# A hybrid decoder step on one core: decay banks written by kind, the last head's old states read in the gate stage, states in head order, stored SiLUs one at a time

## The chip, the core and the metric

The kernel is one program on one core of a Trainium2 chip. The metric is the device time of one execution in microseconds (us), as the median of the runs. The engines are named as in the profile: PE is TensorE with its matmuls (PEld its weight loads), DVE is VectorE, ACT is ScalarE, POOL is GpSimd, and SP is the engine whose instruction queue issues most of the DMAs here. Each engine takes its instructions in the order of its own queue, and waits in front of an instruction until what it needs is there.

## What is computed

One inference step of a two-layer decoder trunk, for one prompt of 512 tokens and eight samples of 8 tokens: 576 token columns, carried together. Layer 0 is a gated short convolution, layer 1 an mLSTM block with four heads of width 512. Everything is in float32. The part that matters here is layer 1 after its projections:

```
gates = concat([q, k, v]) @ w_if + b_if           # input gate ig, log forget gate logf, per head
b = cumsum(logf);  logD = where(causal, b[i] - b[j] + ig[j], -inf)
m_row = maximum(b + m, max(logD));  w_inter = exp(b + m - m_row)
S = (q @ k.T) * exp(logD - m_row)                 # decayed scores
num = w_inter * (q @ C) + S @ v                   # C: the old state, 512 x 512 per head and sample
den = w_inter * (q @ n) + sum(S)
h = num / maximum(abs(den), exp(-m_row))
C_new = decay * C + kw.T @ v                      # written out for every head and sample
out = ((layernorm(h) * onorm) + skip * xc) * silu(z);   y = out @ w_out
```

The prompt starts from a zero state, so only the samples have old states `C`: 4 heads x 8 samples x 512 x 512 floats, 33.6 MB, which are read for `q @ C`, read again, updated and written.

## The kernel before

Large products are made in three passes of split operands: an operand is cut into a rounded part `hi` (a cast on ACT) and a remainder `lo` (a subtraction on DVE), and PE adds hi*hi, hi*lo and lo*hi. `products` and `step` (the matmuls of line 235) do this for one 1024-deep block of weights; `split_weights` (lines 215 and 216) cuts the weights, which the SP queue loads (line 221). One tile of the gate path z, made by `z_tile`, is 48 such matmuls of 256 or 320 columns. The 16 z tiles serve as filler for PE through the whole last part: `z_tile(pops)` takes a list of places in the tile at which the next entry of the Python list `work` is run. A scheduler of the language then orders each engine's queue by its own estimate of the times.

The stages that matter, in the order of the code at the end of `trunk`:

1. **Gate stage.** `gate_rows` makes the decay rows on DVE and ACT; `scores` and `sample_scores` make the score matrix of head 2 (the other heads' scores were made earlier and stored), `gate_columns` turns the rows into columns (line 1079 and on). PE works on z tiles meanwhile.
2. **Decays.** `decay_scores(h, t)`, t = 0, 1, 2, writes the logarithms of the decay factors of one head into one PSUM bank `d` each, as mask plus one-hot products: a mask matmul (`masks`, 128 x 128, lines 1109 and 1117) puts -BIG where nothing may be seen, a matmul with a one-hot of 48 rows (`pick`, lines 1110, 1112 and 1118) adds the row values. ACT takes the exponential (lines 1113 and 1119), DVE multiplies it into the scores (line 1122). Heads 0 and 1 come ahead of the first numerators, heads 2 and 3 in the stage of head 0.
3. **Heads.** For each head: `numerators` (lines 1285 and 1286), `weighted_keys`, `final_state`, then z tiles with `preps` of the next head, and `head_out` of this head: a transpose into a bank (line 1364, `hb` at line 1355), a scaled copy on ACT (lines 1358 and 1366), and the product with silu(z) on DVE (lines 1369 and 1370).
4. **States.** A stream of 64 pieces (`piece`, one 512 KB half of a unit; a unit is a head, a group of four samples and a quarter of the rows) runs beside stages 2 and 3. Its clock counts PE work, one piece per 3.45 us. A piece makes two update matmuls `r` (line 1231), DVE adds them to the state `c` (line 1232), and SP stores it (line 1201). The heads come in the order 2, 0, 1, 3. Six buffers of 512 KB hold the loaded states (line 178).

**Reading old states** (`query_state`, matmuls of line 857 into the bank `qa`): heads 3, 0 and 1 do this earlier, beside the projections, with loads of their own (`unit`, `meet`). Head 2 does it in the stream: `piece` calls `query_state` with the state that it has loaded for the update anyway, eight units in all. The bank `qa` is one of the four banks of the tag `b1`, which `r`, `d`, `s`, `pn`, `ha` and `hb` share.

**SiLU.** Exponentials and SiLU need different tables of ACT. Until `silu_table` loads the second one (line 991), z tiles are copied raw (line 979) and listed in `raw_z`; `head_out` then applies SiLU to a stored tile in place (`silu`, line 986). The instruction is only told to come after the table load:

```
        def silu(out, src):
            with tc.issue_after(table[0]):
                last_silu[:] = [nc.scalar.activation(out, src, AF.Silu).ins]
```

Of the kernel before, what the change touches and what calls it, by code (L numbers as in the profile page):

```python
# [22 lines left out]
NP = 512  # L23
# [44 lines left out]
def trunk(tc, io):  # L68
    nc = tc.nc
    ctx = ExitStack()  # L70
    with ctx:
# [81 lines left out]
        def col(name, i=0):  # L153
            return cols[:, COLS[name] + i:COLS[name] + i + 1]
# [826 lines left out]

        table, last_silu, raw_z = [], [], []

        def silu(out, src):
            with tc.issue_after(table[0]):
                last_silu[:] = [nc.scalar.activation(out, src, AF.Silu).ins]  # L986
# [113 lines left out]
        def decay_scores(h, t):  # L1100
            eye = masks[:, 0:128]

            def onehot(r):
                return pick[:, r:r + 1].broadcast_to([48, P])

            blocks = ((0, 0, 512, 0), (1, 0, 384, 1), (1, 384, 512, 3), (2, 0, 256, 2))
            d, e = bank("d"), T(512, name="e")
            for _, a, b, jt in [x for x in blocks if x[0] == t]:
                nc.tensor.matmul(d[:, a:a + 128], eye, masks[:, 128:256], start=True, stop=False)
                nc.tensor.matmul(d[:, a:a + 128], onehot(4 * h + jt), Rs[0:48, 128 * jt:128 * jt + 128], start=False, stop=True)  # L1110
                if jt < 3:
                    nc.tensor.matmul(d[:, a + 128:b], onehot(4 * h + jt), Rs[0:48, 128 * jt + 128:NP], start=True, stop=True)
                last_exp[:] = [nc.scalar.activation(e[:, a:b], d[:, a:b], AF.Exp, bias=G["p"][:, jt, 4 * h + jt:4 * h + jt + 1])]
            if t == 2:
                for u in range(2):
                    s = slice(256 + 128 * u, 384 + 128 * u)
                    nc.tensor.matmul(d[:, s], eye, masks[:, s], start=True, stop=False)
                    nc.tensor.matmul(d[:, s], onehot(4 * h), Rp[0:48, :], start=False, stop=True)
                    last_exp[:] = [nc.scalar.activation(e[:, s], d[:, s], AF.Exp, bias=G["s"][:, 1 + u, 4 * h:4 * h + 1])]
            if h not in Sc:  # L1120
                Sc[h] = fetched.pop(("S", h))
            nc.vector.tensor_tensor(Sc[h][t], Sc[h][t], e, ALU.mult)
# [57 lines left out]

        ORDER = (2, 0, 1, 3)
        units = [(h, u, dt) for h in ORDER for u in range(2) for dt in range(4)]
# [23 lines left out]
        def piece(n):  # L1206
# [4 lines left out]
            if i == 0:  # L1211
# [10 lines left out]
                if dt == 3 and j:  # L1222
                    key_stack(*j)
                if h == 2:
                    query_state(st, [halves[n], halves[n + 1]], 4 * u + dt)
            load_half(n + 2)
# [119 lines left out]
        def head_out(h, et):  # L1346
# [18 lines left out]
            o = y2[f]  # L1365
            nc.scalar.activation(o[:, 0:NP], pa, AF.Copy, scale=col("onorm", f))
            x, = fetched.pop(("x", f))
# [41 lines left out]
        fetch_stack(0)  # L1409
        fetch_stack(2)  # L1410
        fetch(("ks", 2, 0), copies(kss[2], 0))
        load_half(0)
        load_half(1)
        gate_rows()
        st = heads[2]
        work.extend(lambda dt=dt: scores(st, dt) for dt in range(4))
        work.extend(lambda u=u: sample_scores(st, u) for u in range(2))
        z_tile((2, 5))
        z_tile((1, 3, 5, 7))
        value_stack(0)  # L1420
        value_stack(2)
        work.append(gate_columns)
        z_tile((4,))
        clock[:] = EARLY, EARLY
# [15 lines left out]
        for h in range(NH):  # L1440
# [38 lines left out]
            else:  # L1479
# [4 lines left out]
                z_tile((1, 3, 5, 7))  # L1484
                if h == 2:
                    finish(h)
                sample_numerators(h)
# [227 lines left out]
```

## Time and profile before

| | us |
|---|---|
| median of 3 runs (1643.87 to 1644.4) | 1644.11 |
| the profiled execution, its own time | 1649.75 |
| its span in the profile | 1648.0 |
| PE busy (98% of the span) | 1620.8 |
| DVE busy (68%) | 1118.0 |
| ACT busy (49%) | 807.7 |

The profiled execution took 5.64 us more than the median run, and its time lies 1.75 us above its span. Durations below are from this one execution. Times in the trace are counted from the span's start. PE being busy means that some matmul is in its pipeline; it doesn't tell how fast it streams. The granted clock (PEclk) says that: 1.00 is 2.4 GHz and 0.50 is 1.2 GHz.

### The profile page before, as it was taken

To read this page: it belongs to the slowest core of one execution; us is meant where nothing else is said; L and a number is where in the kernel's file an instruction comes from. 1 tells how busy PE (TensorE), PEld (TensorE's weight loads), DVE (VectorE), ACT (ScalarE), POOL (GpSimd) and SP (SyncE) were. 2 spreads that over 40 slices of the span, in tenths; PEclk is the share of its full clock that TensorE was granted. 3 is DMA by queue.
4 is the path that set the end of the run, shared out by engine and by line. 5 is a ranking of instruction groups with operands and counts; after the bars stand their busy time and mean duration, and the time that the engine had idled before them with its cause. 6 is when DMAs were issued, how large, how long until landed. Compare 5 with 4: busy or idle time off the path is not lost. (4 is left out here: it accounts for less than half of the span.)

```text
span 1648.0 us, 31023 instructions
## 1 busy us (share of the span) xinstructions
PE 1620.8 (98%) x11997; PEld 1546.6 (94%) x11997; DVE 1118.0 (68%) x2124; ACT 807.7 (49%) x1622; POOL 136.2 (8%) x263
## 2 busy tenths in 40 slices
PE   9999999999999999999999999999999998998998
PEld 8999999999999999999999999998998787998997
DVE  6988888885337975655966456455468667778765
ACT  5566666653234554434645344344455556555431
POOL 1111111110000000000011010101002000000000
PEclk9999999999999999999999999999999899999999
DMA  6477776754333434434534454553656687998982
GB/s 219 110 166 175 169 170 165 175 132 145 131 114 92 142 120 134 138 119 154 168 99 141 159 180 152 155 182 125 200 182 216 225 274 274 329 351 287 339 330 104
DMA packets 115748, 298.46 MB, mean 181 GB/s; under 512 B 12656, under 2 KB 28912, under 8 KB 115600
## 3 DMA queue, kind: packets, MB, share of 16 engines
q1 hardware_dynamic: 92176, 264.47, 48.7%
q0 software_dynamic: 8064, 14.68, 6.0%
q10 hardware_dynamic: 15360, 17.32, 3.1%
q8 instruction: 94, 1.54, 0.4%
q14 instruction: 54, 0.44, 0.1%
HBM read 235.91 MB, written 60.52 MB: 180 GB/s over the span
## 5 line engine op out<-in xcount | busy, mean ns | idle before, releaser
L345 PE MATMUL p<-hi,wh 128*128 128x288 f32 x1540 | 453.8, 296 | 1.9 <-ACT wh L264 1.1
L345 PE MATMUL p<-lo,wh 128*128 128x288 f32 x1540 | 452.6, 295 | 0.0
L345 PE MATMUL p<-hi,wl 128*128 128x288 f32 x1540 | 450.9, 295 | 0.2 <-DVE wl L265 0.2
L345 PEld LDWEIGHTS p<-hi,wh 128*128 128x128 f32 x1540 | 288.3, 188 | 12.9 <-DVE ws L350 6.6
L345 PEld LDWEIGHTS p<-lo,wh 128*128 128x128 f32 x1540 | 289.0, 188 | 0.0
L345 PEld LDWEIGHTS p<-hi,wl 128*128 128x128 f32 x1540 | 288.0, 188 | 0.4 <-DVE wl L265 0.4
L264 ACT CAST wh<-wr 128x512 fp32r<-128x512 f32 x298 | 171.4, 578 | 215.1 <-PE p L345 121.7
L265 DVE TENSOR_TENSOR wl<-wr,wh 128x512 fp32r<-128x512 f32 x298 | 185.0, 634 | 91.0 <-ACT wh L264 89.7
L235 PE MATMUL acc<-hi,wh 128*128 128x256 f32 (+1 forms) x1072 | 234.9, 299 | 4.5 <-ACT num L1298 3.2
L235 PE MATMUL acc<-hi,wl 128*128 128x256 f32 (+1 forms) x1072 | 232.2, 298 | 0.0
L235 PE MATMUL acc<-lo,wh 128*128 128x256 f32 (+1 forms) x1072 | 232.2, 298 | 0.0
L264 ACT CAST wh<-ws 128x512 fp32r<-128x512 f32 (+1 forms) x201 | 114.9, 573 | 193.8 <-PE p L345 120.4
L215 ACT CAST wh<-wr 128x512 fp32r<-128x512 f32 x170 | 104.8, 619 | 199.2 <-PE acc L235 144.3
L235 PEld LDWEIGHTS acc<-hi,wh 128*128 128x128 f32 x1072 | 181.5, 191 | 10.2 <-ACT num L1298 3.4
L216 DVE TENSOR_TENSOR wl<-wr,wh 128x512 fp32r<-128x512 f32 x170 | 116.5, 688 | 100.2 <-ACT wh L215 88.0
L235 PEld LDWEIGHTS acc<-hi,wl 128*128 128x128 f32 x1072 | 180.6, 190 | 1.6 <-issue 1.3
L235 PEld LDWEIGHTS acc<-lo,wh 128*128 128x128 f32 x1072 | 180.7, 190 | 0.5 <-issue 0.2
L265 DVE TENSOR_TENSOR wl<-ws,wh 128x512 fp32r<-128x512 f32 (+1 forms) x201 | 125.3, 629 | 75.5 <-ACT wh L264 75.0
L1232 DVE SCALAR_TENSOR_TENSOR c<-c,cols,r 128x512 f32<-128x512 f32 x128 | 91.5, 742 | 28.8 <-PE r L1231 26.3
L433 PE MATMUL p<-hi,wh 128*128 128x288 f32 x496 | 109.2, 300 | 0.0
L433 PE MATMUL p<-hi,wl 128*128 128x288 f32 x496 | 107.8, 295 | 0.0
L433 PE MATMUL p<-lo,wh 128*128 128x288 f32 x496 | 106.6, 295 | 0.0
(387 smaller groups left out, 2580.2 us busy)
## 6 DMA issues: line engine op xcount, KB each, us to landing
wr<-wts SPq DMA_DIRECT2D x222, 512.0 KB, 3.6
c<-cs SPq DMA_DIRECT2D x112, 512.0 KB, 6.0
cs_out<-c SPq DMA_DIRECT2D x64, 512.0 KB, 7.0
ws<-wts SPq DMA_DIRECT2D x28, 256.0 KB, 4.5
ws<-wts POOLq DMA_DIRECT2D x28, 256.0 KB, 4.8
wr<-wts POOLq DMA_DIRECT2D x28, 256.0 KB, 4.2
x<-xcs SPq DMA_DIRECT2D x20, 288.0 KB, 5.0
x<-xT SPq DMA_DIRECT2D x16, 288.0 KB, 4.2
```

The costliest lines, as they stand in the source:

```text
L215: last_act[0] = nc.scalar.copy(hi, raw[:, 4 * i:4 * i + 4, :]).ins
L216: nc.vector.tensor_tensor(lo, raw[:, 4 * i:4 * i + 4, :], hi.bitcast(F32), ALU.subtract)
L235: nc.tensor.matmul(acc[:, o:o + j - i], a[:, k % 4, :], x[:, i:j], start=(first and k == 0 and p == 0), stop=(last and k == 7 and p == 2))
L264: last_act[0] = nc.scalar.copy(hi, src).ins
L265: nc.vector.tensor_tensor(lo, src, hi.bitcast(F32), ALU.subtract)
L345: nc.tensor.matmul(bank_, a[:, j, :], x, start=(start and n + j + i == 0), stop=(n == len(groups) - 1 and j == len(g) - 1 and i == 2), ski ...
L433: nc.tensor.matmul(b, a[:, k % 4, :], x[:, t:t + HT], start=bool(start) and k == 0 and i == 0, stop=(k == n - 1 and i == 2), skip_group_ch ...
L1232: ins = nc.vector.scalar_tensor_tensor(ct[:, j, :], ct[:, j, :], dec[:, o + j:o + j + 1], r, ALU.mult, ALU.add).ins
```

## The change

Four edits, all in the last part of layer 1:

- **Decay banks.** `decay_scores` writes all masks of a bank first, then all one-hot products over the bank's whole blocks, then takes the exponentials. Per head 15 matmuls become 11.
- **Last head's old states.** `meet_last` calls `query_state` for head 2 in the gate stage, with loads of its own (`unit(2, ...)`); `piece` no longer does it. The first loads of the stream move behind the last two of these.
- **Head order of the states.** The stream goes 0, 1, 2, 3; the value stack of head 2 is no longer made in the gate stage, and the call that drained head 2's pieces ahead of its numerators is gone.
- **SiLU.** The SiLU of a stored tile is told to come after the last scaled copy of `head_out` (`last_y`, line 1370 of the changed kernel), so one per copy.

```
         def silu(out, src):
-            with tc.issue_after(table[0]):
+            with tc.issue_after(last_y[0] if last_y and out is src else table[0]):
...
             d, e = bank("d"), T(512, name="e")
-            for _, a, b, jt in [x for x in blocks if x[0] == t]:
-                nc.tensor.matmul(d[:, a:a + 128], eye, masks[:, 128:256], start=True, stop=False)
-                nc.tensor.matmul(d[:, a:a + 128], onehot(4 * h + jt), Rs[0:48, 128 * jt:128 * jt + 128], start=False, stop=True)
-                if jt < 3:
-                    nc.tensor.matmul(d[:, a + 128:b], onehot(4 * h + jt), Rs[0:48, 128 * jt + 128:NP], start=True, stop=True)
+            mine = [x for x in blocks if x[0] == t]
+            for i, (_, a, b, jt) in enumerate(mine):
+                nc.tensor.matmul(d[:, a:a + 128], eye, masks[:, 128:256], start=(i == 0), stop=False, skip_group_check=True)
+            if t == 2:
+                nc.tensor.matmul(d[:, 256:512], eye, masks[:, 256:512], start=False, stop=False, skip_group_check=True)
+            for _, a, b, jt in mine:
+                nc.tensor.matmul(d[:, a:b], onehot(4 * h + jt), Rs[0:48, 128 * jt:128 * jt + b - a], start=False,
+                                 stop=(a, t) != (0, 2), skip_group_check=True)
+            if t == 2:
+                for u in range(2):
+                    nc.tensor.matmul(d[:, 256 + 128 * u:384 + 128 * u], onehot(4 * h), Rp[0:48, :], start=False, stop=(u == 1),
+                                     skip_group_check=True)
+            for _, a, b, jt in mine:
                 last_exp[:] = [nc.scalar.activation(e[:, a:b], d[:, a:b], AF.Exp, bias=G["p"][:, jt, 4 * h + jt:4 * h + jt + 1])]
             if t == 2:
                 for u in range(2):
                     s = slice(256 + 128 * u, 384 + 128 * u)
-                    nc.tensor.matmul(d[:, s], eye, masks[:, s], start=True, stop=False)
-                    nc.tensor.matmul(d[:, s], onehot(4 * h), Rp[0:48, :], start=False, stop=True)
                     last_exp[:] = [nc.scalar.activation(e[:, s], d[:, s], AF.Exp, bias=G["s"][:, 1 + u, 4 * h:4 * h + 1])]
...
-        ORDER = (2, 0, 1, 3)
+        ORDER = (0, 1, 2, 3)
...
-                if h == 2:
-                    query_state(st, [halves[n], halves[n + 1]], 4 * u + dt)
...
-            nc.scalar.activation(o[:, 0:NP], pa, AF.Copy, scale=col("onorm", f))
+            last_y[:] = [nc.scalar.activation(o[:, 0:NP], pa, AF.Copy, scale=col("onorm", f)).ins]
...
-        fetch_stack(2)
-        fetch(("ks", 2, 0), copies(kss[2], 0))
-        load_half(0)
-        load_half(1)
+        fetch(("ks", 0, 0), copies(kss[0], 0))
+        st = heads[2]
+        ready = [unit(2, *divmod(i, 4)) for i in range(2)]
+
+        def meet_last(i):
+
+            query_state(st, ready.pop(0), i)
+            if i < 6:
+                ready.append(unit(2, *divmod(i + 2, 4)))
+            else:
+                load_half(i - 6)
+
         gate_rows()
-        st = heads[2]
-        work.extend(lambda dt=dt: scores(st, dt) for dt in range(4))
-        work.extend(lambda u=u: sample_scores(st, u) for u in range(2))
-        z_tile((2, 5))
-        z_tile((1, 3, 5, 7))
+        first = [lambda dt=dt: scores(st, dt) for dt in range(4)] + [lambda u=u: sample_scores(st, u) for u in range(2)]
+        second = [lambda i=i: meet_last(i) for i in range(8)]
+        work.extend([x for p in zip(first, second) for x in p] + second[6:])
+        z_tile((0, 2, 4, 6))
+        z_tile((0, 1, 3, 4, 5, 7))
         value_stack(0)
-        value_stack(2)
         work.append(gate_columns)
-        z_tile((4,))
+        z_tile((0, 1, 2, 4, 6))
...
-                if h == 2:
-                    finish(h)
```

What this does to the queues, at three places. In the rows a name's number tells one tile from another.

**PE, the decay banks of heads 0 and 1 between the last z tile of the gate stage and the first numerators.** `d` are the decay banks, `r` the state updates. Before, from the third bank of head 0 on:

```order
L1109 MATMUL d_15838<-masks_15293 128x128
L1110 MATMUL d_15838<-Rs_15285,pick 128x128
L1109 MATMUL d_15869<-masks_15293 128x128
L1110 MATMUL d_15869<-Rs_15285,pick 128x128
L1112 MATMUL d_15869<-Rs_15285,pick 128x128
L1109 MATMUL d_15919<-masks_15293 128x128
L1110 MATMUL d_15919<-Rs_15285,pick 128x128
L1112 MATMUL d_15919<-Rs_15285,pick 128x384
```

And now, from the second bank of head 0 on:

```order
L1110 MATMUL d_15888<-masks_15293 128x128 x2
L1114 MATMUL d_15888<-Rs_15285,pick 128x384
L1114 MATMUL d_15888<-Rs_15285,pick 128x128
L1235 MATMUL r_15905<-vst_15672,km_15848 128x512
L1235 MATMUL r_15909<-vst_15672,km_15849 128x512
L1110 MATMUL d_15918<-masks_15293 128x128
L1112 MATMUL d_15918<-masks_15293 128x256
L1114 MATMUL d_15918<-Rs_15285,pick 128x256
L1118 MATMUL d_15918<-Rp_15286,pick 128x128 x2
```

Masks and one-hots took turns within a bank; now a bank has one run of each. Ten updates `r` stand ahead of the first numerator where eight did, and 42 of the 48 matmuls of the fifth z tile stand ahead of the first update where 23 did.

**SP, the loads of the gate stage.** `c` are halves of states, `wr` weights of z tiles, `ld` fetched stacks. Before:

```order
L1143 DMA ld_15361<-vss_7298 128x1x512
L1143 DMA ld_15363<-kss_7302 128x1x512
L178 DMA c_15365<-cs 128x1024
L178 DMA c_15367<-cs 128x1024
L221 DMA wr_15761<-wts 128x1024
L178 DMA c_15805<-cs 128x1024
L178 DMA c_15854<-cs 128x1024
L221 DMA wr_15903<-wts 128x1024
L178 DMA c_15946<-cs 128x1024
L178 DMA c_16014<-cs 128x1024
L1039 DMA m_out<-t_15272 16x576
```

And now, from the third unit of head 2 on, with what each waits for:

```order
L178 DMA c_15479<-cs 128x1024 [waits DMAHW7_49]
L178 DMA c_15481<-cs 128x1024 [waits DMAHW0_49]
L221 DMA wr_15817<-wts 128x1024 [waits DMAHW1_49,Activation_49]
L221 DMA wr_15950<-wts 128x1024 [waits DMAHW2_49,DVE_49]
L178 DMA c_15531<-cs 128x1024 [waits DMAHW4_49,DMAHW3_49,PE_49]
L178 DMA c_15533<-cs 128x1024 [waits PE_49]
L178 DMA c_15590<-cs 128x1024 [waits DMAHW6_49,DMAHW5_49,PE_49]
L178 DMA c_15592<-cs 128x1024 [waits PE_49]
L1039 DMA m_out<-t_15272 16x576 [waits DMAHW7_49,DVE_49]
```

Six halves were loaded ahead, without a wait for PE, and stayed for the stream. Now three units are loaded ahead, and from the fourth on a load waits until PE has read an older unit.

**ACT, behind the load of the SiLU table.** `z` are gate tiles, `y` outputs of `head_out`, `wh`, `vh`, `hi`, `sth` casts. Before:

```order
L991 ACT_TABLE_LOAD
L986 ACTIVATE z_15524<-z_15524 128x576
L986 ACTIVATE z_15639<-z_15639 128x576
L986 ACTIVATE z_15734<-z_15734 128x576
L986 ACTIVATE z_15894<-z_15894 128x576
L986 ACTIVATE z_16029<-z_16029 128x576
L986 ACTIVATE z_16335<-z_16335 128x576
L986 ACTIVATE z_16643<-z_16643 128x576
L1133 CAST sth_16702<-ld_15900 128x256
L215 CAST wh_17232<-wr_17226 128x512
```

And now:

```order
L991 ACT_TABLE_LOAD
L986 ACTIVATE z_15541<-z_15541 128x576
L215 CAST wh_17148<-wr_17142 128x512
L1254 CAST vh_16640<-ld_16453 128x512
L1255 CAST vh_16640<-cst 128x2
L979 COPY z_16654<-acc_16541 128x576
L1254 CAST vh_16656<-ld_16455 128x512
L1255 CAST vh_16656<-cst 128x2
L215 CAST wh_17234<-wr_17232 128x512
```

Seven SiLUs followed the table load in a row; now one does, and three more stand singly between the scaled copies further down. The table load itself stands earlier: one and a quarter z tiles of matmuls (60) are still to come on PE behind the last decay bank, where 15 were.

## Rows read from the trace of the kernel before

**Rows 1.** Part 1 of the page: busy time, share of the span, instructions.

```profile
PE 1620.8 (98%) x11997; PEld 1546.6 (94%) x11997; DVE 1118.0 (68%) x2124; ACT 807.7 (49%) x1622; POOL 136.2 (8%) x263
```

**Rows 2.** Busy time by stretch: PE, PEld, DVE, ACT, POOL, PEclk, DMA share, GB/s.

```profile
1250.80:1283.90 33.10, 33.10 (x249) 32.40 (x247) 28.25 (x63) 20.62 (x46) 2.40 (x6) 1.00 0.55 191
1283.90:1297.30 13.40, 13.35 (x73) 7.71 (x72) 5.90 (x9) 4.44 (x10) 0.22 (x1) 0.99 0.31 113
...
1297.30:1307.40 10.10, 9.69 (x29) 7.42 (x30) 7.99 (x14) 6.02 (x14) 0.18 (x1) 0.51 0.89 281
...
1360.20:1371.30 11.10, 7.30 (x45) 5.01 (x44) 7.25 (x12) 10.79 (x23) 0.00 (x0) 0.88 0.86 300
1371.30:1375.40 4.10, 4.07 (x19) 4.07 (x20) 4.10 (x8) 2.33 (x5) 0.18 (x1) 0.50 0.46 170
```

**Rows 3.** The same view, stretches cut by what the DMA engines do.

```profile
1240.00:1262.00 22.00, 22.00 (x162) 18.65 (x161) 14.19 (x26) 9.04 (x19) 4.04 (x13) 1.00 1.00 356
1262.00:1297.00 35.00, 35.00 (x241) 29.32 (x240) 25.23 (x57) 19.72 (x43) 2.62 (x7) 1.00 0.32 106
...
1340.00:1606.00 266.00, 253.34 (x1777) 236.25 (x1777) 197.16 (x377) 134.15 (x280) 8.97 (x22) 0.97 0.91 320
```

**Rows 4.** Chain that ended last, decay banks: start, us, engine, tile, line.

```profile
1294.37 0.06 PE d L1109
1294.43 0.25 PE d L1110
1294.68 0.26 PE d L1109
...
1295.19 0.11 PE d L1112
...
1303.43 0.21 PE num L1285
```

**Rows 5.** The same chain: a meeting, updates after a meeting and alone, z matmuls, transposes.

```profile
1283.94 0.99 PE qa L857 x8
1284.94 0.43 PE r L1231
...
1307.85 0.23 PE r L1231
...
1399.72 12.80 PE acc L235 x96
...
1494.77 0.44 PE ha L1364 x4
```

**Rows 6.** Groups by line on DVE, costliest first: busy time, mean ns, idle before.

```profile
L1232 DVE SCALAR_TENSOR_TENSOR c<-c,cols,r 128x512 f32<-128x512 f32 x128 | 91.5, 742 | 28.8 <-PE r L1231 26.3 <-DMA cs_out<-c 1.9 <-DMA c<-cs 0.5
...
L1122 DVE TENSOR_TENSOR ld<-ld,e 128x512 f32<-128x512 f32 x9 | 6.2, 688 | 4.5 <-ACT e L1113 4.5
```

**Rows 7.** Timeline of ACT around the table load: start, us, line, operation, idle before.

```profile
1352.07 0.62 ACT L215 CAST wh<-wr 128x512 fp32r<-128x512 f32 x1
1352.59 0.62 ACT L1250 CAST vh<-ld 128x512 fp32r<-128x512 f32 x1
...
1360.21 1.28 ACT L991 ACT_TABLE_LOAD   x1
1361.50 4.13 ACT L986 ACTIVATE z<-z 128x576 f32<-128x576 f32 x7
...
1368.17 0.68 ACT L1366 ACTIVATE y<-ha,cols 128x512 f32<-128x512 f32 x1
...
1370.64 0.64 ACT L986 ACTIVATE z<-acc 128x576 f32<-128x576 f32 x1
```

**Rows 8.** Timeline of PE in the same stretch.

```profile
1365.59 0.66 PE L1364 MATMUL ha<-cst,num 128*128 128x128 f32 x4 [0.84 <-DVE c L1232]
1368.90 2.10 PE L1364 MATMUL ha<-cst,num 128*128 128x128 f32 x8 [2.66 <-ACT y L1366]
```

**Rows 9.** DMA issues between 1240 and 1300: count, size, median us to landing.

```profile
c<-cs SPq DMA_DIRECT2D x7, 512.0 KB, 10.0
```

More of the change, by code (lines that the diff above doesn't have):

```diff
@@ L980, in z_tile @@
             zs[f // 4].append(z)
-        table, last_silu, raw_z = [], [], []
+        table, last_silu, raw_z, last_y = [], [], [], []
         def silu(out, src):
-            with tc.issue_after(table[0]):
+            with tc.issue_after(last_y[0] if last_y and out is src else table[0]):
                 last_silu[:] = [nc.scalar.activation(out, src, AF.Silu).ins]
```

## The prediction, made before the changed kernel was run

> **What bounds the kernel now.** I read the page first. PE is busy for 98% of the span [rows 1], so time can only come from PE: from matmuls that disappear, from stretches in which PE stands idle or streams slowly, or from work that moves into such stretches. Then I read busy time by stretch over the part that the change touches [rows 2], and three stretches stand out. From 1250.8 to 1283.9 PE is busy throughout at clock 1.00. From 1297.3 to 1307.4 it is busy too, but the granted clock is 0.51, its lower level of 1.2 GHz; what it did in the 13.4 us before was thin, 73 matmuls where the 33.1 us before that had 249. From 1360.2 to 1371.3 PE is busy for 7.30 of 11.10 us while ACT is busy for 10.79, and the 4.10 us behind it run at clock 0.50. Last I read the DMA by stretch [rows 3]: full from 1240 to 1262 (share 1.00, 356 GB/s), nearly idle from 1262 to 1297 (0.32), and from 1340 to 1606 at 0.91.
>
> **Decay banks.** The chain shows the price of taking turns [rows 4]: a mask behind a one-hot takes 0.26 us, a one-hot behind a mask 0.25 us, but a one-hot of the same 128 columns behind another one-hot 0.11 us, and a mask behind matmuls of full height 0.06 us. I take 0.05 us for each 128 columns more, and 0.05 us for one that follows its own kind. Before, a head costs 0.73 (t = 0), 1.2 (t = 1) and 1.6 us (t = 2), 3.5 us in all. Now it costs about 0.26 + 0.41, then 0.26 + 0.05 + 0.36 + 0.05, then 0.26 + 0.11 + 0.30 + 0.10: 2.15 us. That is 1.35 us a head. For heads 2 and 3 the banks stand between z matmuls on a busy PE, so 2.7 us; the last of these banks opens the stretch in which ACT decides (below), so I count 2.3 us. For heads 0 and 1 it falls into the stretch before the first numerators, which is worked out next. If the 0.25 us were the price of adding onto columns written just before, rather than of changing from 128 to 48 rows, the change would save only the merged matmuls, some 0.4 us a head. The mask's 0.26 us in a fresh bank, where nothing is added, speaks for the change of rows. The Trainium skill (TensorEngine Tiling (Array Packing), Key Properties) says that changing the tiling mode drains TensorE; by that rule it is the number of changes that counts, 12 a head before and 6 now, and these rows agree with it.
>
> **Meetings of head 2 in the gate stage.** A meeting of one unit takes 0.99 us, and the matmul behind it 0.43 instead of 0.23 us [rows 5], so 1.2 us. Eight of them, 9.6 us, now come ahead of the first update instead of three. Before, the first meeting starts at 1283.94, with 23 matmuls of the fifth z tile done; now 42 are done by the first update, 19 more at 0.133 us (12.80 us for 96) or 2.5 us. The first update then starts at 1283.9 + 2.5 + 9.6 = 1296.0. From there to the first numerator PE has ten updates (2.3 us), six z matmuls and two heads of decays, 7.4 us. DVE has more: ahead of the first remainder that the numerators need, its queue holds eight updates of 0.74, five products of 0.69 [rows 6], one weight remainder and that first remainder, which I take at 0.69 too: 10.8 us. So DVE decides, and the first numerator comes at about 1307.1 instead of 1303.4 [rows 4], 3.7 us later. By then five more meetings (6.0 us) and two more updates (0.5 us) are done than before. The gain is 2.7 us; I take off 0.5 us for meetings that wait a little for their loads and count **2.2 us**. If the DVE queue should not decide, PE's 7.4 us do, and the gain is 6 us. The wait that the clock shows at 0.51 before will show here again, since PE is idle for some 3 us of this stretch.
>
> The extra loads are 16 halves of 512 KB, 8.4 MB, which the kernel before did not make. They fall mostly into 1250 to 1285; 1262 to 1297 had a DMA share of 0.32 [rows 3], and its free 0.68 of 35 us at 356 GB/s hold 8.5 MB. The meetings also leave the bank `qa`, one of four, free for the stretch from the first update on; I count that as nothing, because DVE and ACT free the other three as fast as they are filled.
>
> **SiLUs singly.** Before, ACT loads the table in 1.28 us, then runs seven SiLUs in 4.13 us, 0.59 each; the first scaled copy that frees a bank comes at 1368.17, and the SiLU that frees the z tile's bank ends at 1371.28 [rows 7]. PE waits 0.84 and 2.66 us in front of transposes meanwhile [rows 8]. It loses 3.8 us idle, then half of 4.10 us at clock 0.50 [rows 2], about 6 us with what is slow inside the stretch. Now, from the last decay bank to the SiLU that frees the bank, ACT's queue holds: three exponentials (0.9), the table (1.28), four stored SiLUs (2.4), one z copy and the last SiLU (1.1), eleven casts of 512 columns at 0.52 (1352.07 to 1352.59) or 5.7, two of 256 (0.6), six small copies (0.5), three scaled copies of 0.58 and four small ones of 0.2 (2.6): 15.1 us. (The exponentials, narrow casts and small copies are estimates by their width from the rows of their wide kin.) PE has 60 z matmuls (8.0 us), four updates (0.9), five groups of transposes at 0.44 (2.2) and the first numerator's matmuls (0.7): 11.8 us. So PE still waits, 3.3 us in place of 3.8, now in one place, before the second numerator; the four SiLUs that stay ahead and the casts are what is late next. I take the clock behind it as halved for about half as long as before. The gain is **2.0 us**, between nothing (ACT has the same work, only in another order) and 6 us (no wait is left).
>
> **Head order, value stack.** The order of the heads moves no matmul, and the queues behind head 0 keep their order but for names. Nothing there is on the path.
>
> **The sum.** 2.2 + 2.3 + 2.0 = 6.5 us. Against its own time the profiled execution would be 1649.75 - 6.5 = 1643.25 us. That execution lies 5.64 us above the median; the same 6.5 us from the median of 1644.11 give **1637.6 us**. A measurement of this kernel can tell about 0.2%, 3.3 us, from no change: faster is below 1640.8, slower above 1647.4.
>
> **Rivals.**
>
> - *More than that goes.* If DVE does not decide before the first numerator (6 instead of 2.2), and one SiLU between copies is enough (6 instead of 2.0), the gain is 14 us and the time 1630. For it: both waits are a few us, and the clock gives half of any idle stretch back. Against it: the sums of the two queues above. Chance 0.22.
> - *The state stream takes it back.* From 1340 to 1606 the DMA share is 0.91 [rows 3]. If PE reaches each piece earlier, and loads and stores cannot follow, the updates wait for them and most of the gain is gone; 1642 to 1644. Against it: the change shortens the time ahead of 1376 only, the pieces follow PE work and not time, and the DMA has idle shares there. The same time results if ACT's stretch gains nothing and the decays save only the 0.4 us a head. Chance 0.18.
> - *The meetings wait for their loads; slower.* A load from the fourth unit on is issued only when PE has left a buffer, and half-unit loads took 10.0 us to land in this stage [rows 9]. PE passes three units in about 11 us. From 11 us of landing on, each round of three buffers makes PE wait, in front of z matmuls that are ready: at 15 us two rounds cost 8 us, and the low clock behind them 2 us more. With the other 4.3 us gained that is 1650. For it: DMA is full until 1262, and two z weights stand between the loads on SP. Against it: from 1262 on hardly anything else is loaded. [...] Chance 0.10.
>
> **How the numbers follow.** The forecast, 1633 to 1640.8, has 0.50. With the first rival faster has 0.72, the same 0.18, slower 0.10. The range for 8 in 10 runs from 1629 (the first rival, a little beyond) to 1646 (all of the second, and the edge of the third).
>
> **What would show it.** The groups of the page: 44 matmuls of lines 1110 to 1118 in all, and one-hots at 0.1 us or less behind their own kind. The timeline: eight `qa` groups between about 1256 and 1287 without an idle PE ahead of them; the first update near 1296, the first numerator near 1307, with PE idle and DVE full between, and the clock at its lower level there. Behind the table load one SiLU, and one wait of about 3 us of PE for ACT. The prediction is wrong if PE waits for `c` loads in the gate stage, if the first numerator comes before 1303, if no wait for ACT is left behind the table load, or if a new wait for `c` or `cs_out` appears after 1376.

## The result, and the profile after

The changed kernel takes 1636.52 us (median of 5 runs, 1634.36 to 1637.82). The kernel before, on the same chip, takes 1644.11 us (1641.36 to 1648.73). The ratio is 0.9955 with a 95% interval of 0.9944 to 0.9966; the medians differ by 7.6 us. The forecast was 1637.6 us, from 6.5 us of gain.

The profiled execution of the changed kernel took 1636.74 us (span 1634.9). Part 1 of its page answers to [rows 1]:

```profile
span 1634.9 us, 31031 instructions
...
PE 1610.5 (99%) x11981; PEld 1540.3 (94%) x11981; DVE 1117.4 (68%) x2124; ACT 807.0 (49%) x1622; POOL 139.3 (9%) x263
```

PE is busy 10.3 us less with 16 instructions fewer. The chain that ended last shows the meetings and the first numerators (start, us, engine, tile, line), answering to [rows 4] and [rows 5]:

```profile
1256.84 0.99 PE qa L857 x8
...
1284.06 1.00 PE qa L857 x8
...
1295.30 0.23 PE r L1235
...
1303.31 2.00 PE r L1235 x4
1305.31 0.21 PE num L1289
...
1305.74 1.19 PE r L1235 x2
1306.93 0.21 PE num L1289
```

All eight meetings stand between 1256.84 and 1285.06 and the first update comes at 1295.30. The first numerator comes at 1305.31, where [rows 4] has 1303.43: 1.9 us later. After two more updates the numerators go on from 1306.93. The view of busy time by stretch (length, PE busy, clock, DMA share, GB/s) answers to [rows 2]; its last two rows are the stretches in which the kernels below differ most:

```profile
1250.80:1283.90 33.10, 33.10 (x240) 1.00 0.91 323
1284.10:1296.00 11.90, 11.90 (x90) 1.00 0.87 308
1296.00:1300.70 4.70, 4.70 (x23) 0.96 0.59 194
1300.70:1306.80 6.10, 6.10 (x18) 0.50 1.01 336
...
1296.00:1320.00 24.00, 23.73 (x134) 0.86 0.89 296
...
1488.00:1526.00 38.00, 35.64 (x252) 1.00 0.89 318
```

PE has no idle time among the meetings although the DMA share there rose from 0.55 to 0.91. The clock is at its lower level (1.2 GHz) for 6.1 us inside the fourth row's bounds, 6.8 us in all; before it was 10.2 us. PE has no idle time in the third and fourth row either. The last two stretches in the kernel before:

```profile
1296.00:1320.00 24.00, 23.54 (x132) 0.79 0.93 309
...
1488.00:1526.00 38.00, 33.41 (x221) 0.91 0.83 282
```

The second row of before has 4.6 us of idle time and a lower clock in a place that no line of the change touches; the fourth numerators, of head 3, stand there.

Behind the table load, which now comes at 1348.11, ACT's timeline answers to [rows 7]:

```profile
1346.51 0.47 ACT L1121 ACTIVATE e<-d,colp 128x256 f32<-128x256 f32 x1
1346.89 0.62 ACT L1125 ACTIVATE e<-d,cols 128x128 f32<-128x128 f32 x2
...
1348.11 1.28 ACT L991 ACT_TABLE_LOAD   x1
1349.40 0.69 ACT L986 ACTIVATE z<-z 128x576 f32<-128x576 f32 x1
...
1356.20 0.62 ACT L215 CAST wh<-wr 128x512 fp32r<-128x512 f32 x1 [1.36 <-PE acc L235]
...
1361.42 0.71 ACT L1370 ACTIVATE y<-ha,cols 128x512 f32<-128x512 f32 x1
1361.99 0.71 ACT L986 ACTIVATE z<-z 128x576 f32<-128x576 f32 x1
...
1362.77 0.69 ACT L986 ACTIVATE z<-acc 128x576 f32<-128x576 f32 x1
```

What PE waited for between 1340 and 1380 (us in total, times, longest) answers to [rows 8]:

```profile
PE num L1289 <- ACT z L986: 3.4, 1, 3.4
PE ha L1368 <- ACT y L1370: 1.5, 1, 1.5
```

The SiLUs stand singly, but PE waits 4.9 us for ACT here, where before it waited 3.8 us (2.7 and 0.3 for ACT, 0.8 for DVE).

### The profile page after: what moved, and what is told of

Its sections match the earlier page's. It is cut to its first block, busy times and chain, and to the rows that moved or that the text cites. A ratio compares the mean times of both kernels' runs of the same rounds, so it can differ in the third digit from the quotient of the medians.

```text
span 1634.9 us, 31031 instructions
## 1 busy us (share of the span) xinstructions
PE 1610.5 (99%) x11981; PEld 1540.3 (94%) x11981; DVE 1117.4 (68%) x2124; ACT 807.0 (49%) x1622; POOL 139.3 (9%) x263
## 5 line engine op out<-in xcount | busy, mean ns | idle before, releaser
L1236 DVE SCALAR_TENSOR_TENSOR c<-c,cols,r 128x512 f32<-128x512 f32 x128 | 90.7, 741 | 16.5 <-PE r L1235 13.9
```

Of the source, the lines that this page charges most:

```text
L1236: ins = nc.vector.scalar_tensor_tensor(ct[:, j, :], ct[:, j, :], dec[:, o + j:o + j + 1], r, ALU.mult, ALU.add).ins
```

## The experiments

In the labels and the table D stands for the decay banks, M for meetings with head order, S for SiLUs singly. **How the table is made:** each profile was cut into pieces of half a microsecond by the view of busy time by stretch. "Idle" is length less PE's busy time. "Low" is the time at the lower clock, 2 x (1 - clock) x length. "Work" is the time that passed, less idle, less half of low: what PE would have taken without waiting and at full clock. Part 1 runs from 1240 to the last second numerator (of head 1), part 2 from there to the last sample numerator of head 3. Behind part 2 all profiles take 121 us. "Profiled" is the profiled execution's own time. The last column is the granted clock over the whole span, as the median of a kernel's runs; for before it is that of its runs beside the experiments.

| kernel | part 1: work | idle | low | of it, at the first numerators | part 1 ends | part 2: work | idle | low | profiled | median | ratio | clock |
|---|---|---|---|---|---|---|---|---|---|---|---|---|
| before | 128.9 | 4.5 | 17.1 | 10.2 | 1381.9 | 133.4 | 8.2 | 6.8 | 1649.75 | 1644.11 | | 0.994 |
| before again | 129.6 | 4.5 | 17.1 | 10.2 | 1382.7 | 134.4 | 6.4 | 0.0 | 1646.32 | 1644.00 | 1.0003 | 0.994 |
| D | 125.2 | 5.3 | 23.9 | 13.7 | 1382.4 | 134.1 | 6.1 | 3.4 | 1647.25 | 1647.18 | 1.0013 | 0.991 |
| M | 124.9 | 5.0 | 23.9 | 17.1 | 1381.8 | 132.9 | 5.5 | 3.4 | 1644.70 | 1643.81 | 1.0002 | 0.991 |
| S | 127.7 | 4.4 | 17.1 | 10.2 | 1380.6 | 132.0 | 7.5 | 6.8 | 1646.17 | 1645.50 | 1.0006 | 0.994 |
| D+M | 123.5 | 5.9 | 6.8 | 0.0 | 1372.9 | 133.2 | 12.2 | 6.8 | 1644.42 | 1647.33 | 1.0019 | 0.9935 |
| D+S | 126.0 | 5.8 | 10.2 | 3.4 | 1376.8 | 133.1 | 6.1 | 3.4 | 1640.41 | 1641.63 | 0.9988 | 0.9935 |
| M+S | 126.0 | 3.7 | 17.1 | 13.7 | 1378.3 | 132.8 | 11.1 | 10.2 | 1650.02 | 1650.02 | 1.0033 | 0.991 |
| changed kernel | 121.3 | 5.5 | 13.7 | 6.8 | 1373.6 | 133.9 | 4.8 | 3.4 | 1636.74 | 1636.52 | 0.9955 | 0.996 |
| full-height one-hots in before | 122.4 | 7.2 | 17.1 | 6.8 | 1378.2 | 133.6 | 6.2 | 6.8 | 1644.17 | 1644.09 | 1.0000 | 0.993 |
| M+S, full height | 122.5 | 6.1 | 3.4 | 0.0 | 1370.2 | 133.8 | 10.6 | 6.8 | 1640.81 | 1641.69 | 0.9987 | 0.995 |
| D+M, early key stack | 122.1 | 5.3 | 10.2 | 3.4 | 1372.5 | 131.8 | 7.9 | 17.1 | 1643.33 | 1643.34 | 0.9999 | 0.993 |
| changed, early key stack | 122.3 | 5.6 | 13.7 | 6.8 | 1374.7 | 133.7 | 6.1 | 0.0 | 1637.54 | 1636.22 | 0.9954 | 0.9955 |
| changed, full height | 120.8 | 8.1 | 6.8 | 0.0 | 1372.4 | 133.7 | 6.3 | 6.8 | 1638.49 | 1637.77 | 0.9961 | 0.995 |

That the split holds is seen in part 2: the time spent there differs by 9 us between kernels, the work only by 2.6 us. The two profiles of before differ by 0.7 us in the work of part 1, and a difference of that size tells nothing. Both profiles of before lie above its median (5.6 and 2.3 us), so a usual execution of it waits less than its two rows show.

The last column says how far a profile stands for the other runs. (1 - clock) x span is half of all the low time of a run: 9.9 us in the median run of before, 14.8 in that of D, M and M+S, 10.7 in that of D+M and 6.5 in that of the changed kernel. The clocks are given to 0.001, which is 1.6 us. So D and M lose some 5 us more than before to the low clock in their usual runs too, and of the 7.6 us that the changed kernel gains some 3.4 are the clock's.

### Each part alone, and the kernel before again

The kernel before, not edited:

> The kernel before, unchanged, for a second profile. Its profiled execution shown with the prediction lay 5.6 us above the median, and between 1487 and 1550 us it lost 5 us against the changed kernel, in a place that the change does not touch (a wait for a state load, then z matmuls at half clock). Theory 1: that was a peculiarity of one execution; the ratio is 1.000 (within 0.002), and in this profile the way from the second half of head 2 to that of head 3 is shorter than the 63.6 us of before, near 58.6. Theory 2: it is how this kernel always runs there, 63 us again, and then part of the gain of 7.6 us is made behind 1487.

Ratio 1.0003 (0.9992 to 1.0014). From the second half of head 2 to that of head 3 it took 59.6 us, 4 us less than in the first profile. Theory 1 holds: about 4 us of what the first profile of before and that of the changed kernel differ by is one execution's wait in part 2, and is not the change's gain.

D, the hunk on lines 1107 to 1127 alone, cut to its core:

```diff
-                nc.tensor.matmul(d[:, a:a + 128], eye, masks[:, 128:256], start=True, stop=False)
-                nc.tensor.matmul(d[:, a:a + 128], onehot(4 * h + jt), ...
+            for i, (_, a, b, jt) in enumerate(mine):
+                nc.tensor.matmul(d[:, a:a + 128], eye, masks[:, 128:256], start=(i == 0), ...
+            for _, a, b, jt in mine:
+                nc.tensor.matmul(d[:, a:b], onehot(4 * h + jt), ...
```

> The kernel before with the decay banks alone written as masks, then one-hots, then exponentials. Theory (changing between 128 and 48 rows is what costs): t = 0 to 2 of a head cost 2.15 us in place of 3.5; heads 2 and 3 lie beside z matmuls on a busy PE, heads 0 and 1 before the first numerators, where DVE may hide them: 2.3 to 5.4 us faster, ratio 0.9967 to 0.9986. Rival (adding onto columns just written is what costs): one-hots stay at 0.2 us or more also behind their own kind, 0.4 us a head: ratio 0.9995 or nearer to 1.

Ratio 1.0013 (1.0001 to 1.0025): neither; if anything slower. The work fell by 4.0 us against the mean of the two profiles of before (125.2 against 129.25), as the theory wants. But the first numerators, which start 3 us earlier (1300.4), run at the lower clock until 1311, 3.5 us longer than before, and a second low stretch of 3.4 us follows at 1331: together that costs 3.4 us, and idle grew by 0.8.

S alone:

```diff
-            with tc.issue_after(table[0]):
+            with tc.issue_after(last_y[0] if last_y and out is src else table[0]):
```

> The kernel before with the SiLUs of stored z tiles alone issued behind the scaled copies instead of all behind the table load. Theory: ACT's queue still decides, PE waits 3.3 us in one place in place of 3.5 in two, some of the half clock behind it goes: 2 us faster, ratio 0.9988. Rival 1: ACT has the same work in another order, nothing is gained: 1.000. Rival 2: the order is all that made PE wait there, the second numerator comes 6 us earlier: 0.9964.

Ratio 1.0006 (0.9995 to 1.0018): rival 1. Idle time and clock in part 1 are those of before.

M alone, with the head order, cut to its core:

```diff
-        ORDER = (2, 0, 1, 3)
+        ORDER = (0, 1, 2, 3)
-                if h == 2:
-                    query_state(st, [halves[n], halves[n + 1]], 4 * u + dt)
+            query_state(st, ready.pop(0), i)
+        second = [lambda i=i: meet_last(i) for i in range(8)]
```

> The kernel before with the meetings of head 2 in the gate stage and the states in head order, decay banks and SiLUs as before. Theory: five meetings and two updates more stand before the first numerator, which comes 3.7 us later than the 1303.4 of before (DVE's queue decides): 2.2 us faster, ratio 0.9987. Rival 1: the first numerator comes no later, 6 us faster: 0.9964. Rival 2: head order and the longer state stream take it back, or the meetings wait for their loads: 1.000 or above, with PE idle ahead of the qa groups.

Ratio 1.0002 (0.9993 to 1.0011), the number of rival 2 without its cause: PE is not idle ahead of the meetings, and the state stream is no slower (in part 2, idle and half of low make 7.2 us, among the least). The first numerator comes at 1307.99 in the chain, 4.6 us later than before, again with no idle time of PE between the meetings and it. The work fell by 4.35 us; the low clock took 3.4 of it, 17.1 us of it at the first numerators, where the view by stretch has, for D:

```profile
1296.00:1320.00 24.00, 23.14 (x111) 0.72 0.97 331
```

and for M:

```profile
1296.00:1320.00 24.00, 24.00 (x99) 0.64 0.78 268
```

against 0.79 and 132 matmuls before. So two of the three parts do take away what was forecast or more, and lose most of it again to the clock in these 24 us or just behind them.

### Two parts together

Each is the changed kernel with one hunk undone. D+M (the S line above undone):

> The changed kernel with the SiLUs of stored tiles behind the table load as before: decay banks and meetings (with the head order) together. Each of the three parts alone gained nothing (ratios 1.0013, 1.0006, 1.0002), all together gain 7.6 us. Theory: decays and meetings need each other, through the clock at the first numerators: its low stretch there lasted 10.2 us before, 13.7 with the decays alone, 17.1 with the meetings alone and 6.8 in the changed kernel; here it should be 6.8 again, the first numerators end near 1315, and the ratio is 0.996 to 0.997, SiLUs singly being worth 0 to 2 us on top. Rival: the SiLUs are what the other two need; then this one is at 0.999 or above.

Ratio 1.0019 (1.0009 to 1.0028). In the profile the half of the theory that speaks of the clock holds: no low clock at the first numerators, part 1 ends at 1372.9, 9 us ahead of before. The ratio falls to the rival all the same. In the profile part 2 loses 15.6 us (12.2 idle, half of 6.8 low), 4 more than the first and 9 more than the second profile of before. This execution is not a usual one: its clock, 0.995, is the highest of the twelve runs (0.989 to 0.995), and it took 2.9 us less than their median. Where a usual run loses these 2.9 us no profile shows. The views of D+M by stretch and of PE's waits from 1488 to 1526:

```profile
1488.00:1526.00 38.00, 30.40 (x198) 0.91 0.83 286
```
```profile
PE acc L235 <- ACT num L1302: 4.3, 1, 4.3
```

Its chain names what ACT stood behind:

```profile
1504.05 6.47 DMA ld<-kss
...
1511.17 0.58 ACT num L1302
1511.80 4.69 PE acc L235 x18
```

The load of head 3's first key stack was issued at 1504.05 and landed 6.47 us later; the copy of a numerator bank stood behind its scaling in ACT's queue, and the 18 z matmuls behind it ran at half speed. In the changed kernel, which is at the same point of its work at the same time, the same chain reads:

```profile
1495.73 3.55 DMA cs_out<-c
1499.30 0.33 SPq L178
1499.68 5.25 DMA ld<-kss
1504.95 0.38 ACT ld L1138
...
1505.58 0.58 ACT num L1302
1506.20 2.66 PE acc L235 x18
```

The links are the same: a state store frees a state buffer, the load of the next state half (line 178) has waited for it on SP, the key stack stands behind that load, ACT behind the key stack, PE behind ACT. Here it is issued 4.4 us earlier, PE waits 1.0 us, and the 18 matmuls take 2.66 in place of 4.69 us. The wait of z matmuls for ACT at this place is no peculiarity of D+M: it is 3.2 and 1.7 us in the two profiles of before, and 4.4 in M+S.

D+S (meetings and order undone):

> The kernel before with decay banks and SiLUs changed, meetings and head order as before. Theory (clock at the first numerators): as with the decays alone, 13.7 us at the low level there and numerators that start 3 us earlier but run at half speed; ratio 1.000 to 1.002. Rival: decays and SiLUs are the pair that gains; ratio 0.996 to 0.998.

Ratio 0.9988 (0.9977 to 1.0). Its low clock at the first numerators was 3.4 us, not 13.7: the theory's number is missed, and the ratio lies between the two. Added to D, S gains: 1.0013 falls to 0.9988, with intervals that do not meet. D and D+S have the same instructions in the same order on every engine up to the SiLUs, yet one profile has 13.7 us of low clock there and the other 3.4. The order alone therefore does not fix that length. The twelve runs of D+S lie between 1638.31 and 1648.05 us, and the fastest has the highest clock (0.996), the slowest the lowest (0.989).

M+S (decay banks undone):

> The changed kernel with the decay banks as before: meetings, head order and SiLUs. Theory (clock at the first numerators): as with the meetings alone, some 17 us at the low level there; ratio 0.999 to 1.001. Rival: meetings and SiLUs are the pair that gains; ratio 0.996 to 0.998.

Ratio 1.0033 (1.0021 to 1.0045), slower than the theory's range. The low stretch is long as expected (13.7 us); part 2 then lost 16.2 us (11.1 idle, half of 10.2 low), as in D+M.

### What a decay bank pays for

One-hots and their rows over 128 partitions with zeros, everything in the order of before:

```diff
-        Rs, Rp, pick = R(name="Rs"), R(128, name="Rp"), const.tile([48, 16], F32R, name="pick")
+        Rs, Rp, pick = R(name="Rs"), R(128, name="Rp"), const.tile([P, 16], F32R, name="pick")
-                nc.tensor.matmul(d[:, a:a + 128], onehot(4 * h + jt), Rs[0:48, 128 * jt:128 * jt + 128], ...
+                nc.tensor.matmul(d[:, a:a + 128], onehot(4 * h + jt), Rs[:, 128 * jt:128 * jt + 128], ...
```

> The kernel before, with the one-hots and the rows they pick from written over 128 partitions in place of 48, zeros below, so that no matmul of a decay bank changes its height. Same order as before, masks and one-hots taking turns. Theory (the change between 128 and 48 rows is what costs): a one-hot of 128 columns behind a mask takes 0.06 to 0.11 us in place of 0.25, a mask behind a one-hot 0.06 in place of 0.26, a head's banks 1.6 us in place of 3.5. Rival (adding onto columns just written costs): the one-hot behind its mask stays at 0.2 us or more. The time itself can go either way, since the first numerators' clock decides more than the 2 to 7 us of the banks: 0.996 to 1.002.

Ratio 1.0000 (0.9991 to 1.0009). PE's timeline (start, us, line, tile, shapes) settles the price:

```profile
1294.64 0.22 PE L1109 MATMUL d<-masks 128*128 128x128 f32 x1
1294.70 0.27 PE L1110 MATMUL d<-Rs,pick 128*128 128x128 f32 x1
1294.81 0.33 PE L1112 MATMUL d<-Rs,pick 128*128 128x256 f32 x1
1294.98 0.22 PE L1117 MATMUL d<-masks 128*128 128x128 f32 x1
1295.05 0.27 PE L1118 MATMUL d<-Rp,pick 128*128 128x128 f32 x1
```

Read the starts: a mask takes 0.06 us until the one-hot begins, the one-hot on the columns just written 0.11 us until the next, a mask behind a one-hot of 256 columns begins 0.17 us after it. In [rows 4] the same steps cost 0.26 and 0.25 us. It is the change of height that costs, not the adding. The work fell by 6.9 us, more than D takes away. Idle time took 2.7 of it in part 1, and by the medians nothing is left; of the other 4 us some 1.6 are the clock's by the last column; where a usual execution of before makes up the rest on this one, no profile shows.

The same edit in M+S, in place of the new order of the banks:

> Meetings and SiLUs changed (ratio 1.0033 alone), the decay banks in the order of before, but with one-hots and rows over 128 partitions, so that they cost little without the new order. Theory: what the new decay banks do for the meetings is to make the stretch before the first numerators short and dense enough that the clock stays low for 0 to 7 us in place of 13.7; any other edit that takes the changes of height away does the same: low stretch at most 7 us there, first numerators end near 1315 in place of 1320, ratio 0.995 to 0.998. Rival: the new order itself is what counts (or chance); ratio 1.000 or above.

Ratio 0.9987 (0.9977 to 0.9997) against 1.0033 without it. The theory's steps hold: no low clock at the first numerators, which end at 1313.8, and part 1 ends 11.7 us ahead of before, the earliest of all. The view by stretch, of this kernel:

```profile
1296.00:1320.00 24.00, 22.73 (x157) 1.00 0.83 282
```

157 matmuls where M alone had 99. The ratio misses the range by a little, since part 2 gives 14.0 us away (10.6 idle, half of 6.8 low). So with the meetings early, cheap banks go with a shorter low stretch, whichever way they are made cheap: 17.1 and 13.7 us with the old banks (M, M+S), 0, 3.4, 6.8 and 6.8 with the new order, 0 and 0 at full height. Each is one execution, and D and D+S differ by 10.3 us there with the same order, so this is a pattern and no proof; the clock over all runs goes the same way, 0.991 with the old banks and 0.993 to 0.996 with cheap ones.

### The key stack earlier

The load of head 3's first key stack, moved from the units' second half to the middle of the first:

```diff
+                if (h, u, dt) == (ORDER[2], 0, 2):
+                    fetch(("ks", ORDER[3], 0), copies(kss[ORDER[3]], 0))
                 if dt == 0 and j:
-                    fetch(("ks", *j), copies(kss[j[0]], j[1]))
+                    if m != 6:
+                        fetch(("ks", *j), copies(kss[j[0]], j[1]))
```

> Decay banks and meetings together (ratio 1.0019 in the run before this one), and the load of head 3's first key stack issued four update pieces of two units earlier, in the middle of the units of head 2 instead of with their second half. Theory: decays and meetings had gained 9 us by the end of the second numerators (1372.9 against 1381.9), and lost it again at 1507, where ACT's queue stands behind the stack that this load brings (landed at 1510.5), PE waits 4.3 us and then runs 6.8 us at the low clock. With the load early that wait goes: from the fourth numerators to the sample numerators of head 3 20 to 22 us in place of 28.7, and a ratio of 0.995 to 0.997. Rival (the state stream bounds this part whatever the order of its loads): the wait moves to the next load or store and the ratio stays at 1.000 or above.

Ratio 0.9999 (0.9991 to 1.0008) against 1.0019: 4 us came back by the medians (1647.33 to 1643.34), not the 8 to 11 us expected, and from the fourth numerators to the sample numerators it takes 25.5 us. The wait for ACT is gone, but the rival has the larger share: in the profile part 2 loses 16.5 us (7.9 idle, half of 17.1 low), no less than the 15.6 of D+M. By the view by stretch (PE, PEld, DVE, ACT, POOL, clock), DVE is full and PE waits for it:

```profile
1488.00:1496.00 8.00, 8.00 (x61) 7.88 (x61) 8.00 (x14) 7.15 (x13) 0.22 (x1) 1.00 0.65 204
1496.00:1504.00 8.00, 5.25 (x22) 3.24 (x20) 8.00 (x13) 0.74 (x2) 0.00 (x0) 0.77 0.77 252
1504.00:1511.00 7.00, 6.76 (x30) 6.30 (x31) 6.25 (x13) 1.85 (x4) 0.55 (x3) 0.53 0.98 334
```

DVE is busy for all 16 us; PE runs 22 matmuls in the second row, and the clock falls. The changed kernel in the same stretch also has DVE full, but spreads PE's work, 51 and 53 matmuls, and keeps its clock:

```profile
1488.00:1496.00 8.00, 7.27 (x51) 6.73 (x50) 8.00 (x14) 3.62 (x7) 0.53 (x1) 1.00 0.82 268
1496.00:1504.00 8.00, 7.67 (x53) 6.67 (x53) 8.00 (x13) 1.65 (x3) 0.37 (x2) 1.00 0.71 245
```

Both edits in the changed kernel itself:

> The changed kernel with the same load early. Its own wait at that place was 1.0 us with no low clock behind it. Theory: 0 to 1.5 us less than the changed kernel, ratio 0.9945 to 0.9960, and executions that lie closer together. Rival: the load takes a place on SP's queue and a buffer from something that is needed sooner; ratio above 0.997.

Ratio 0.9954 (0.9941 to 0.9968): the theory's range, but no difference from the changed kernel that can be told.

> The changed kernel with one-hots and rows over 128 partitions. Theory: six changes of height a head are gone, some 0.15 us each, up to 0.9 us a head, of which half lies before the first numerators, where DVE's queue decides: 1 to 3 us less than the changed kernel, ratio 0.994 to 0.9955. Rival: no gain (the first numerators wait for DVE, and what follows waits for the state loads): 0.9955 or above.

Ratio 0.9961 (0.9948 to 0.9974): the rival. Work fell by 0.5 us more and the clock stayed up at the first numerators, but idle grew from 5.5 to 8.1 us in part 1, and part 2 lost 9.7 in place of 6.5 us. No version tried is faster than the changed kernel by more than its measurement can tell.

## Why the prediction was right

The time and the sign came out, but the sum was right in total rather than in its terms, and that the total came so near was in part luck.

- **Meetings: the place was right, the wait was wrong.** Forecast: first update at 1296.0, no idle PE among the meetings. Measured: 1295.30, none. But then DVE was to decide, PE to stand idle for some 3 us, and the first numerator to come at 1307.1, 3.7 us later than before. It comes at 1305.31, 1.9 us later, and PE is not idle at all between 1250.8 and 1306.8. The forecast added up DVE's queue to the first remainder `lo` and compared it with the first numerator of before, which needs no remainder. The first product that needs one, in the kernel before and in the changed kernel:

```profile
1305.42 0.41 PE L1285 MATMUL num<-vh,lo 128*128 128x256 f32 x1
```
```profile
1307.34 0.39 PE L1289 MATMUL num<-vh,lo 128*128 128x256 f32 x1
```

  That is 1.9 us later too. And DVE waited for PE, 1.0 us; its timeline in the changed kernel:

```profile
1304.07 0.75 DVE L1236 SCALAR_TENSOR_TENSOR c<-c,cols,r 128x512 f32<-128x512 f32 x1 [1.00 <-PE r L1235]
...
1306.60 0.68 DVE L167 TENSOR_TENSOR lo<-ld,hi 128x512 fp32r<-128x512 f32 x1
```

  For this `lo` only a weight load waited, 0.3 us, while PE went on. What filled the 10.0 us from the first update to the first numerator is PE's own work: 7.4 us by the forecast's own sum, and 2.5 us more because 5.0 of the 10.0 us ran at the lower clock (0.75 over this stretch). That this clock "will show here again, since PE is idle" was right in the clock and wrong in the reason: it fell with PE busy, here as in the kernel before (13.35 of the 13.40 us ahead of it in [rows 2]). By the forecast's count, 6.5 us more work done and the first numerator 1.9 us later, the gain up to there is 4.6 us in place of 2.7; the banks of heads 0 and 1 are a part of it. With the old banks the low stretch lasts 17.1 us in place of 10.2, and M alone gains nothing: the 2.2 us were not there without the new banks.
- **Decay banks: the mechanism was right, the place wrong.** Changes of height are the price; the runs at full height show it. After the change the last bank of head 3 starts at 1345.60 and the next z matmul at 1346.41; the timeline of PE in the changed kernel:

```profile
1345.60 0.22 PE L1110 MATMUL d<-masks 128*128 128x128 f32 x1
1345.66 0.34 PE L1112 MATMUL d<-masks 128*128 128x256 f32 x1
1345.92 0.38 PE L1114 MATMUL d<-Rs,pick 48*128 48x256 f32 x1
1346.14 0.33 PE L1118 MATMUL d<-Rp,pick 48*128 48x128 f32 x2
```

  That is 0.8 us for t = 2, as forecast (0.26 + 0.11 + 0.30 + 0.10). The step that failed is that heads 0 and 1 count nothing, because DVE would hide them, and heads 2 and 3 2.3 us. D removes 4.0 us of work, and as PE is what decides ahead of the first numerators, heads 0 and 1 count as well. The first numerators end at 1315.2 with it and at 1320.4 without it (the changed kernel against M+S); of these 5.2 us 3.4 are half the difference of the low stretches.
- **SiLUs: the 2.0 us do not exist where they were counted.** Forecast was one wait of 3.3 us in place of 3.8; there are two, 4.9 us. The SiLU that frees the z bank ends at 1363.46, 17.0 us after ACT takes up the last decay bank (1346.51; forecast 15.1), and ACT itself waited 1.4 us of them for PE: its queue was added up nearly right. The low clock behind the waits lasts 6.9 us with and without the change and was not halved. From the last sample numerator of head 0 to the end of part 1 it takes 58.4 us in the changed kernel and 58.6 in D+M, so S is worth about nothing there. What S changes shows 130 us later: it changes the order in which loads, stores and DVE's products are queued from the SiLUs on. Added to M it costs (1.0002 to 1.0033), added to D+M it gains 10.8 us (medians of 1647.33 and 1636.52, from two sets of runs), of which some 4 are the clock's by the last column of the table.
- **The second rival was real, though not in the changed kernel.** "The state stream takes it back" had a chance of 0.18, with the argument against it that pieces follow PE's work and not time. In D+M, M+S and M+S at full height 14 to 16 us are idle or half lost in part 2, against 6.5 in the changed kernel; one link of it, followed in D+M, is the queue on SP with the key stack behind a state load, which the prediction did not name. It is not the whole: with the key stack early D+M got 4 of the 10.8 us back, and PE waited for DVE instead. Why the changed kernel keeps clear of these waits is not shown.
- **The sum.** Work 129.25 to 121.3 is 7.95 us; idle and half of low in part 1 went from 13.0 to 12.35; part 2 lost 6.5 us, like the second profile of before (6.4). That makes 8.6 us up to 1374, and 7.6 by the medians. The forecast of 6.5 came near because errors cancelled: it counted too little for the decay banks, 2.0 us for the SiLUs that are not there, and nothing for the shorter low clock, some 3.4 us by the medians.

**Left open:** what makes the low stretch at the first numerators last 13.7 us in D and 3.4 in D+S, or 0 in D+M and 6.8 in the changed kernel, with the same instructions in the same order. In the 4.7 us from 1296.0 on PE was busy throughout in M, the changed kernel and D+M alike, with 25, 23 and 24 matmuls; the clock fell at their end in the first two and stayed up in the third. Each is one profiled execution, and it was not tried to hold the clock there by other means. Open too is why S helps: by the profiles it lowers what part 2 loses only when added to D and M together (15.6 to 6.5 us); added to D it leaves 7.8 as it was, added to M it raises 7.2 to 16.2. No rule behind this is shown.

## What to carry to other kernels

Count a change in two sums: the work that it takes from the bound engine, and the waiting and low clock around it. In this kernel the first came to 4.0, 4.35 and 1.55 us for the parts alone and 7.95 together, while the second ate all of it, by the medians, for each part alone, so a part that measures as nothing alone need not be worth nothing. Look far behind the edit for the next in-order queue in which a late load holds up something that PE needs: here D+M lost in such queues, 130 us later, the 9 us by which its profile was ahead; one late key-stack load on SP was a part of it, and moving it gave 4 us back. And where the order of queues is made by a scheduler, measure the combination.

## What was not expected of the hardware

- The same instructions in the same order, up to the SiLUs, ran with a low-clock stretch of 13.7 us in one kernel and 3.4 in another (D, D+S), 17.1 and 13.7 (M, M+S), 0 and 6.8 (D+M, changed). The low stretch began while PE showed hardly any idle time: 0.5 us in the 24 us of before, none in M. A PE that the profile shows as busy throughout did not keep its clock.
- A matmul that changes between 48 and 128 rows begins some 0.15 us later than one that does not (0.25 against 0.11 us, 0.26 against 0.06 to 0.17), at the clock of 1.00, and the array counts as busy meanwhile.
